# Where the modulation blocks of layer 0 are loaded: two buffers of their own, or these and four of a later stream

## The chip, the cores and the metric

The kernel runs on one core of a Trainium2 chip. The metric is device time in microseconds (us), the median of the runs shown. The engines are TensorE (PE; its weight loads are listed as PEld), VectorE (DVE), ScalarE (ACT), GpSimd (POOL) and SyncE (SP), which here only issues transfers. Each engine, and SP's queue, takes its instructions strictly in the order in which the built program has them.

## The reference

It is a four-layer diffusion transformer on 256 tokens and 256 context tokens of width 2048, in float32. Each layer has a modulation of its own:

```python
def ada_modulation(cond, w, b):
    m = jax.nn.silu(cond) @ w + b          # w: 2048 x 6144 per layer
    return jnp.split(m, 3, axis=-1)        # shift, scale, gate
...
h  = rms_norm(x, norm_g[i]) * (1.0 + scale[:, None, :]) + shift[:, None, :]
hc = rms_norm(ctx, norm_g[i]) * (1.0 + scale_c) + shift_c
...
def fourier_mix(h, w_in, w_out):           # layers 0 and 3
    u, z = jnp.split(h @ w_in, 2, axis=-1)
    ...                                    # 2D FFT of u, times silu(z)
    return y @ w_out
x = x + gate[:, None, :] * o
```

Layer 1 is a windowed attention, layer 2 a convolution block. What matters here is layer 0: no product with its `w_in` can start before the shift and scale of the channels that it contracts over are there, and these need 2048 rows of the modulation matrix.

## The kernel before

**Products.** Matrices are multiplied in split float32: a piece of weights (two row blocks of 128, 512 columns, 512 KB) is loaded into one of two `raw` buffers, ACT writes its high part `whi` (L181), DVE the remainder `wlo` (L182), both in two buffers each, and PE does three matmuls (high by high, high by low, low by high: L194 to L196 where the weights stand still, L214 to L216 where the activations do). Results collect in four PSUM banks named `accz` or `accu`.

**Layer 0, first half (L674 to L728).** The product for z is made in nine steps over the contraction: steps 0 and 1 take one block of 128 channels, steps 2 to 8 two (`steps`, L606). Within a step a loop over four column groups (`cg`) loads one piece, multiplies it into the four banks `accz`, and DVE adds each bank to a sum `y` in SBUF (L726); the next group's matmuls may write a bank only after that. In the last step ACT puts silu on `y` (L728). Then come the 32 pieces of the product for u (`accu`), which starts in the order of its row blocks.

**Layer 0's modulation blocks.** While step j runs, the shift and scale of the channels of step j + 1 are made (`ada_tiles`, L221): in each column group one quarter q of the 2048 rows, 512 rows by 512 columns, 1 MB, is loaded by two transfers (L231) and multiplied by the conditioning vectors (L235, four matmuls on four column strips of the array). After the fourth quarter the sums are turned into columns (L241, L243, L246, L249) and the activations `hh`, `hl` of step j + 1 are built (L448 to L450). The quarters go through two buffers of 1 MB (tile `aw` of the pool `aw0`), which are given back after the last step; step 0 alone puts its second half elsewhere (below).

**The later modulation rows.** All other shifts, scales and gates are made by two streams (`Stream`, L318) from row blocks of 128 rows by 2048 columns, each loaded as two tiles of 512 KB (L331) into four buffers (tile `aw` of the pool `wp`, `AWB` = 4). Stream `ada_v` works on DVE: it multiplies a tile by one number per row and adds it to a running sum `adacc` (L284; the first row block is L282). Stream `ada_a` works on PE (L271). The text of the program starts both in step 8: twelve row blocks (24 tiles) of `ada_v` after the first column group (L721), eight row blocks of `ada_a` in its four groups (L723), and then a part of a row block per piece of the product for u (`pump0`, L731).

**What sets the order.** The program is written as one sequence. A scheduler gives each engine its own order from it; it moves an instruction forward when its inputs and its buffer are free early enough by its own estimate. Buffers of one tile name are handed out in turn in the order of the text. So the 24 tiles of `ada_v`, written in step 8, stand in the queues from step 0 on in the kernel before, since their four buffers have no other user after step 0.

Of the kernel before, what the change touches and what calls it, by code (L numbers as in the profile page):

```python
# [11 lines left out]
F32 = mybir.dt.float32  # L12
# [7 lines left out]
P = 128  # L20
D = 2048
# [39 lines left out]
AWB = 4  # L61
# [7 lines left out]
def dit_kernel(ctx: ExitStack, tc: tile.TileContext, x, c, ctxt, c_ctx, norm_g, ada_w, ada_b,  # L69
               four_w_in, four_w_out, attn_w_in, attn_sink, attn_w_out, conv_w_in, conv_dw_w,  # L70
               conv_dw_b, conv_ln_g, conv_ln_b, conv_w_out, final_g, dft, rope, maskc, out):
    nc = tc.nc
    mm = nc.tensor.matmul
# [3 lines left out]
    wp = ctx.enter_context(tc.tile_pool(name="wp", bufs=1))  # L77
# [11 lines left out]
    def nm(s):  # L89
        uid[0] += 1  # L90
        return f"{s}_{uid[0]}"

    def tmp(shape=(P, 512), dt=F32):
        return wp.tile(list(shape), dt, tag="tmp", bufs=TB, name=nm("tmp"))
# [126 lines left out]
    def ada_tiles(k, n, j, pl, pa):  # L221

        w = 2 * P * n
        for q in range(4):
            if j == 0 and q > 1:
                aw = wp.tile([P, D // 2], F32, tag="aw", bufs=AWB, name=nm("aw"))[:].rearrange("p (k c) -> p k c", k=4)
            else:
                aw = pl.tile([P, 4, 512], F32, tag="aw", bufs=2, name=nm("aw"))
            for i in range(2):
                c0 = (1 - i) * D + P * k  # L230
                nc.sync.dma_start(aw[:, :, i * P * n:(i + 1) * P * n],  # L231
                                  ada_w[0, q * 512:(q + 1) * 512, c0:c0 + P * n].rearrange("(k p) c -> p k c", p=P))
            for g in range(4):
                cs = csil[:, 4 * q + g, :] if q else csil0[:, g, :]
                mm(pa[32 * g:32 * g + cs.shape[-1], :w], cs, aw[:, g, :w],  # L235
                   start=q == 0, stop=q == 3, skip_group_check=True)
            if q < 3:
                yield
        with tc.high_priority(offset=FH if j < FJ else 0):
            a = tmp()  # L240
            nc.scalar.copy(a[:, :w], pa[:, :w])  # L241
            for i in range(2 * n):
                mm(pa[:, 2 * i:2 * i + 2], a[:, i * P:(i + 1) * P], sel[:], start=True, stop=True)  # L243
            for i, c0 in enumerate((16 + k, k)):
                dst = modc[0][:, c0:c0 + n, :]
                nc.vector.tensor_add(dst, pa[:, 2 * n * i:2 * n * (i + 1)].rearrange("p (k o) -> p k o", o=2),  # L246
                                     adabT[:, c0:c0 + n].unsqueeze(2).to_broadcast([P, n, 2]))
                if i == 0:
                    nc.vector.scalar_tensor_tensor(dst, dst, 1.0, ngT[:, k:k + n].unsqueeze(2).to_broadcast([P, n, 2]),  # L249
                                                   op0=ALU.add, op1=ALU.mult)  # L250
        yield
# [356 lines left out]
    def ada_start(j):  # L608
        return ada_tiles(*steps[j], j, aw0, psa_box[0].tile([P, 512], F32, tag="ada", name=nm("pa")))
# [72 lines left out]
    for o in range(2):  # L682
        if o:
            rs[1] = to_channels(1, 512)
        cs = slice(256 * o, 256 * o + 256)
# [105 lines left out]
    for cg in range(4):  # L791
# [9 lines left out]
        if cg == 3:  # L801
            sqrt_table(st.ss[:, 0:1])
            tail = {kt: piece(kt) for kt in range(KT - 4, KT, 2)}
            for o in range(2):
                cs = slice(256 * o, 256 * o + 256)
# [530 lines left out]
```

## Time and profile before

| what | value |
|---|---|
| median of 3 runs | 1928.31 us (1928.18 to 1931.59) |
| the profiled execution, its time | 1930.65 us |
| its span in the trace | 1928.5 us |
| mean granted TensorE clock | 0.986 |
| DVE busy, of the span | 1441.8 us (75%) |
| ACT busy | 892.7 us (46%) |
| POOL busy | 228.0 us (12%) |
| moved by DMA | 433.63 MB, 225 GB/s on average |

The times in the rows count from the start of the span. 2.15 us of the profiled execution's time lie outside of its span. Step 2 of the first half starts at about 71 us, step 8 at about 243 us, the product for u at about 276 us.

A line of the timeline gives start, length, engine, source line, operation, tiles and count, and in square brackets the idle time ahead of it with what ended it. A line of the windows gives, for a stretch, the busy time of each engine, then the granted clock, the busy share of the 16 DMA engines and GB/s. A line of the waits gives engine and line, what it waited for, the sum in us, how often, and the longest. "SPq" rows are SP's queue; DMA landing times run from issue to the last byte.

### The profile page before, as it was taken

Reading aid. Unit: us, or ns where it says so; the run is one execution under the profiler, and the core shown is the slowest. Engines: PE = TensorE matmul, PEld = TensorE weight load, DVE = VectorE, ACT = ScalarE, POOL = GpSimd, SP = SyncE. Lnnn points to the kernel's source line nnn. Section 1 sums busy time; section 2 is a strip of 40 time slices with the busy share of each in tenths; the row PEclk is TensorE's granted clock in tenths of the full one; section 3 lists DMA queues with packets and bytes.
Section 4 is the critical chain, followed back from the end, with each engine's and each line's share of the span. In section 5 each row is a group of like instructions: output and inputs, shape, how many; then the busy total and the mean of one; then the engine's idle time right before and its main releaser. Section 6 shows DMA issues by size and latency. Waiting matters only on the chain.

```text
span 1928.5 us, 30124 instructions
## 1 busy us (share of the span) xinstructions
PE 1852.9 (96%) x11143; PEld 1506.8 (78%) x11143; DVE 1441.8 (75%) x2719; ACT 892.7 (46%) x1606; POOL 228.0 (12%) x127
## 2 busy tenths in 40 slices
PE   6999999999999999999999999899998998999997
PEld 5566657777766787766689887899998887899886
DVE  4899944566654459977897796588899998897675
ACT  6333342224331236465555445444445656556553
POOL 0000000000000000000000002788880002000000
PEclk9999999999999999999999999999998998999999
DMA  8888878666677745831667695476765795876553
GB/s 257 282 297 301 300 245 271 206 232 207 233 269 265 272 151 161 275 120 55 206 208 251 227 320 197 159 232 212 234 230 175 245 322 169 290 273 176 163 175 131
DMA packets 247236, 433.63 MB, mean 225 GB/s; under 512 B 16214, under 2 KB 135734, under 8 KB 247090
## 3 DMA queue, kind: packets, MB, share of 16 engines
q1 hardware_dynamic: 245664, 430.00, 67.5%
q10 hardware_dynamic: 1426, 1.73, 0.3%
q8 instruction: 87, 1.43, 0.3%
q14 instruction: 59, 0.48, 0.1%
HBM read 429.56 MB, written 2.10 MB: 224 GB/s over the span
## 4 chain that ended last, share of the span: by engine, by line
PE 78%; DVE 9%; DMA 6%; issue 3%; ACT 2%; POOL 0%; SPq 0%; DVEq 0%; ACTq 0%; POOLq 0%
PE acco L1040 8%; PE accz L194 6%; PE accz L195 6%; PE accz L196 6%; DMA aw<-in_ada_w_dram 5%; PE acco L1041 4%; PE accu L214 4%; PE accu L215 4%; PE accu L216 4%; PE pa L271 3%; PE accg L194 3%; PE accg L196 3%; PE accg L195 3%; PE acco L194 3%; DVE wlo L182 3%
## 5 line engine op out<-in xcount | busy, mean ns | idle before, releaser
L181 ACT CAST whi<-raw 128x512 fp32r<-128x512 f32 (+1 forms) x764 | 540.8, 758 | 693.0 <-PE accz L195 133.0
L182 DVE TENSOR_TENSOR wlo<-raw,whi 128x512 fp32r<-128x512 f32 x680 | 492.0, 770 | 202.4 <-ACT whi L181 197.7
L182 POOL TENSOR_TENSOR wlo<-raw,whi 128x1024 fp32r<-128x1024 f32 x84 | 203.8, 2434 | 1371.6 <-ACT whi L181 1370.6
L284 DVE SCALAR_TENSOR_TENSOR adacc<-aw,csil,adacc 128x1024 f32<-128x1024 f32 x188 | 243.9, 1302 | 85.7 <-DMA aw<-in_ada_w_dram 85.2
L1040 PE MATMUL acco<-yh,whi 128*128 128x512 f32 x768 | 270.4, 397 | 0.2 <-DVE xT L1048 0.2
L196 PE MATMUL accz<-hx,wlo 128*128 128x256 f32 x768 | 221.1, 289 | 12.1 <-DVE wlo L182 12.0
L195 PE MATMUL accz<-hx,whi 128*128 128x256 f32 x768 | 220.9, 288 | 3.6 <-DVE hx L450 3.6
L194 PE MATMUL accz<-hx,whi 128*128 128x256 f32 x768 | 220.9, 288 | 1.1 <-ACT hx L449 1.1
L1041 PE MATMUL acco<-yh,wlo 128*128 128x256 f32 x768 | 215.2, 280 | 1.2 <-DVE wlo L182 1.2
L1139 DVE SCALAR_TENSOR_TENSOR pv<-gp,dwT,pv 128x256 f32<-128x256 f32 x480 | 191.1, 482 | 24.8 <-ACT pv L1133 24.4
L1040 PEld LDWEIGHTS acco<-yh,whi 128*128 128x128 f32 x768 | 144.1, 188 | 34.6 <-ACT yh L479 0.8
L196 PEld LDWEIGHTS accz<-hx,wlo 128*128 128x128 f32 x768 | 150.1, 196 | 14.1 <-DVE wlo L182 13.1
L195 PEld LDWEIGHTS accz<-hx,whi 128*128 128x128 f32 x768 | 150.3, 196 | 5.4 <-DVE hx L450 4.2
L194 PEld LDWEIGHTS accz<-hx,whi 128*128 128x128 f32 x768 | 150.3, 196 | 3.0 <-ACT hx L449 1.8
L196 PE MATMUL accg<-hx,wlo 128*128 128x256 f32 x512 | 146.6, 286 | 2.8 <-POOL wlo L182 2.7
L194 PE MATMUL accg<-hx,whi 128*128 128x256 f32 x512 | 147.5, 289 | 1.1 <-ACT hx L449 1.1
L1041 PEld LDWEIGHTS acco<-yh,wlo 128*128 128x128 f32 x768 | 144.8, 189 | 2.2 <-DVE wlo L182 2.1
L195 PE MATMUL accg<-hx,whi 128*128 128x256 f32 x512 | 146.4, 286 | 0.0
L194 PEld LDWEIGHTS accg<-hx,whi 128*128 128x128 f32 x512 | 99.6, 195 | 8.5 <-issue 6.9
L194 PE MATMUL acco<-yh,whi 128*128 128x512 f32 (+1 forms) x272 | 105.0, 387 | 0.0
L196 PEld LDWEIGHTS accg<-hx,wlo 128*128 128x128 f32 x512 | 99.6, 195 | 4.3 <-POOL wlo L182 3.4
L195 PE MATMUL acco<-yl,whi 128*128 128x512 f32 (+1 forms) x272 | 102.8, 378 | 0.0
(261 smaller groups left out, 3579.9 us busy)
## 6 DMA issues: line engine op xcount, KB each, us to landing
aw<-in_ada_w_dram SPq DMA_DIRECT2D x376, 512.0 KB, 5.4
raw<-in_four_w_in_dram SPq DMA_DIRECT2D x126, 512.0 KB, 4.6
raw<-in_attn_w_in_dram SPq DMA_DIRECT2D x72, 512.0 KB, 3.6
raw<-in_conv_w_in_dram SPq DMA_DIRECT2D x128, 256.0 KB, 2.9
raw<-in_four_w_out_dram SPq DMA_DIRECT2D x32, 512.0 KB, 6.7
raw<-in_attn_w_out_dram SPq DMA_DIRECT2D x64, 256.0 KB, 4.3
raw<-in_conv_w_in_dram SPq DMA_DIRECT2D x32, 512.0 KB, 4.4
raw<-in_conv_w_out_dram SPq DMA_DIRECT2D x64, 256.0 KB, 4.6
```

Of the source, the lines that this page charges most:

```text
L181: nc.scalar.copy(hv[:, c], iv[:, c])
L182: eng.tensor_sub(lv[:, c], iv[:, c], hv[:, c].bitcast(F32))
L194: mm(o, a, hh, start=st, stop=False, skip_group_check=True)
L195: mm(o, a, hl, start=False, stop=False, skip_group_check=True)
L196: mm(o, b, hh, start=False, stop=kt + k == span[1] - 1, skip_group_check=True)
L214: mm(acc[:], hh, whi[:, k, :], start=st, stop=False)
L215: mm(acc[:], hh, wlo[:, k, :], start=False, stop=False)
L216: mm(acc[:], hl, whi[:, k, :], start=False, stop=kt + k == KT - 1)
L284: ins = nc.vector.scalar_tensor_tensor(acc[:, cs], aw[i][:], cc, acc[:, cs], op0=ALU.mult, op1=ALU.add)
L1040: mm(o[:], whi[:, k, cs], rhs(kt), start=kt == 0, stop=False, skip_group_check=True)
L1041: mm(o[:, :256], wlo[:, k, cs], rhs(kt)[:, :256], start=False, stop=kt == KT - 1, skip_group_check=True)
L1139: nc.vector.scalar_tensor_tensor(pv[:, :256], gt[:, t:t + 256], dwT[:, kt, t:t + 1], pv[:, :256], op0=ALU.mult, op1=ALU.add)
```

## The change

In `ada_tiles` the second half of every step (quarters 2 and 3) now goes into the four 512 KB buffers of the later rows, as step 0's did already; quarters 0 and 1 keep the two buffers of 1 MB. With two channel blocks a quarter takes two of the 512 KB tiles, each loaded by two transfers of 256 KB, so a quarter is four transfers in place of two; with one channel block it still fits in one tile. The matmuls are as many as before and read the tile that holds their row block. No buffer is added.

```diff
         for q in range(4):
-            if j == 0 and q > 1:
-                aw = wp.tile([P, D // 2], F32, tag="aw", bufs=AWB, name=nm("aw"))[:].rearrange("p (k c) -> p k c", k=4)
+            if q > 1:
+                aws = [wp.tile([P, D // 2], F32, tag="aw", bufs=AWB, name=nm("aw"))[:]
+                       .rearrange("p (k c) -> p k c", k=4 // n) for _ in range(n)]
             else:
-                aw = pl.tile([P, 4, 512], F32, tag="aw", bufs=2, name=nm("aw"))
-            for i in range(2):
-                c0 = (1 - i) * D + P * k
-                nc.sync.dma_start(aw[:, :, i * P * n:(i + 1) * P * n],
-                                  ada_w[0, q * 512:(q + 1) * 512, c0:c0 + P * n].rearrange("(k p) c -> p k c", p=P))
+                aws = [pl.tile([P, 4, 512], F32, tag="aw", bufs=2, name=nm("aw"))[:]]
+            r = 4 // len(aws)
+            for h, aw in enumerate(aws):
+                for i in range(2):
+                    c0 = (1 - i) * D + P * k
+                    r0 = q * 512 + h * r * P
+                    nc.sync.dma_start(aw[:, :, i * P * n:(i + 1) * P * n],
+                                      ada_w[0, r0:r0 + r * P, c0:c0 + P * n].rearrange("(k p) c -> p k c", p=P))
...
-                mm(pa[32 * g:32 * g + cs.shape[-1], :w], cs, aw[:, g, :w],
+                mm(pa[32 * g:32 * g + cs.shape[-1], :w], cs, aws[g // r][:, g % r, :w],
                    start=q == 0, stop=q == 3, skip_group_check=True)
```

The change also moves instructions in the queues, since the four buffers now have a user up to the last modulation block of layer 0. Lines behind the diff carry numbers larger by four: L331 is L335, L284 is L288, L726 is L730. Two places are shown here, as the built programs have them; the number behind a tile's name is its own.

SP's queue before, from the last loads of step 7 on: `raw_2065` is the first piece of step 8, `raw_2199`, `raw_2259` and `raw_2319` its other three, `raw_2393` and `raw_2425` the first two pieces of the product for u; `aw` are tiles of later rows.

```order
L157 DMA raw_2065<-in_four_w_in_dram 128x2x512
L331 DMA aw_2164<-in_ada_w_dram 128x1024
L331 DMA aw_2166<-in_ada_w_dram 128x1024
L331 DMA aw_2170<-in_ada_w_dram 128x1024
L331 DMA aw_2172<-in_ada_w_dram 128x1024
L331 DMA aw_2179<-in_ada_w_dram 128x1024
L331 DMA aw_2181<-in_ada_w_dram 128x1024
L157 DMA raw_2199<-in_four_w_in_dram 128x2x512
L157 DMA raw_2259<-in_four_w_in_dram 128x2x512
L157 DMA raw_2319<-in_four_w_in_dram 128x2x512
```

Behind these stand four `aw`, `raw_2393`, four `aw`, `raw_2425`: never more than six tiles of later rows lie between two pieces, and 22 of `ada_v`'s first 24 are ahead of `raw_2065`.

SP's queue of the changed kernel, at the same place of the program: `raw_2107` and `raw_2241` are the first two pieces of step 8, `raw_2301` and `raw_2361` its last two, `raw_2435` and `raw_2467` the first two of the product for u. Between the last two rows stand 30 more loads of L335, `aw_2170` to `aw_2403`, and nothing else.

```order
L157 DMA raw_2107<-in_four_w_in_dram 128x2x512
L335 DMA aw_2139<-in_ada_w_dram 128x1024
L335 DMA aw_2141<-in_ada_w_dram 128x1024
L157 DMA raw_2241<-in_four_w_in_dram 128x2x512
...
L157 DMA raw_2361<-in_four_w_in_dram 128x2x512
L335 DMA aw_2158<-in_ada_w_dram 128x1024
L335 DMA aw_2160<-in_ada_w_dram 128x1024
L335 DMA aw_2164<-in_ada_w_dram 128x1024
L157 DMA raw_2435<-in_four_w_in_dram 128x2x512
L335 DMA aw_2166<-in_ada_w_dram 128x1024
...
L157 DMA raw_2467<-in_four_w_in_dram 128x2x512
```

So the loads of `ada_v` begin with `aw_2139`, behind the first piece of step 8, and 31 tiles of later rows (15 for DVE, 16 for PE) stand between the first and the second piece of the product for u.

DVE before, in step 8, from the remainder of its second piece to that of its third (`accz_2061` to `accz_2064` are the banks of its first column group):

```order
L182 TENSOR_TENSOR wlo_2202<-raw_2199,whi_2201 128x2x128x2 x2
L450 SCALAR_TENSOR_TENSOR hl_355<-tmp_2017,modc_87,hh_354 128x256
L726 TENSOR_TENSOR y_7_363<-accz_2024,y_7_363 128x512
L480 TENSOR_TENSOR dftl_2382<-tmp_2379,dfth_2381 128x512
L726 TENSOR_TENSOR y_0_356<-accz_2061,y_0_356 128x512
L726 TENSOR_TENSOR y_0_356<-accz_2062,y_0_356 128x512
L726 TENSOR_TENSOR y_1_357<-accz_2063,y_1_357 128x512
L480 TENSOR_TENSOR dftl_2382<-tmp_2380,dfth_2381 128x384
L726 TENSOR_TENSOR y_1_357<-accz_2064,y_1_357 128x512
L182 TENSOR_TENSOR wlo_2262<-raw_2259,whi_2261 128x2x128x2 x2
```

DVE of the changed kernel, from the same remainder on (`accz_2103` to `accz_2105` are the first three of these banks):

```order
L182 TENSOR_TENSOR wlo_2244<-raw_2241,whi_2243 128x2x128x2 x2
L730 TENSOR_TENSOR y_7_363<-accz_2066,y_7_363 128x512
L288 SCALAR_TENSOR_TENSOR adacc_2143<-aw_2146,csil,adacc_2143 128x1024
L288 SCALAR_TENSOR_TENSOR adacc_2143<-aw_2148,csil,adacc_2143 128x1024
L288 SCALAR_TENSOR_TENSOR adacc_2143<-aw_2152,csil,adacc_2143 128x1024
L182 TENSOR_TENSOR wlo_2304<-raw_2301,whi_2303 128x2x128x2 x2
L288 SCALAR_TENSOR_TENSOR adacc_2143<-aw_2154,csil,adacc_2143 128x1024
L288 SCALAR_TENSOR_TENSOR adacc_2143<-aw_2158,csil,adacc_2143 128x1024
L288 SCALAR_TENSOR_TENSOR adacc_2143<-aw_2160,csil,adacc_2143 128x1024
L288 SCALAR_TENSOR_TENSOR adacc_2143<-aw_2164,csil,adacc_2143 128x1024
L730 TENSOR_TENSOR y_0_356<-accz_2103,y_0_356 128x512
L730 TENSOR_TENSOR y_0_356<-accz_2104,y_0_356 128x512
```

The multiply-adds of `ada_v`'s first twelve row blocks, which before stand one by one among the work of all steps from step 0 on, now all stand inside step 8, and the additions of its banks stand behind some of them. Behind the second piece of the product for u, the rows of all engines are the same in both programs but for line and tile numbers, up to the end, apart from the places of a few single rows in its first eight pieces.

## The prediction

> **What bounds the kernel now.** I read the page first, then the windows, and then, in the stretch that the change touches, PE's timeline, the waits, SP's timeline and the single lines. The page says that PE is the engine that is nearly always at work:
>
> ```profile
> span 1928.5 us, 30124 instructions
> PE 1852.9 (96%) x11143; PEld 1506.8 (78%) x11143; DVE 1441.8 (75%) x2719; ACT 892.7 (46%) x1606; POOL 228.0 (12%) x127
> ```
>
> The windows of 20 us (busy time of PE, PEld, DVE, ACT, POOL, then granted clock, DMA share, GB/s) show the steps of layer 0, up to about 243 us, and what follows:
>
> ```profile
> 80.00:100.00 20.00, 19.71 (x96) 14.11 (x95) 16.39 (x28) 7.27 (x10) 0.00 (x0) 1.00 0.97 327
> 160.00:180.00 20.00, 19.69 (x100) 13.28 (x99) 18.36 (x25) 6.76 (x7) 0.00 (x0) 1.00 0.91 316
> 240.00:260.00 20.00, 18.65 (x83) 9.78 (x81) 14.84 (x20) 13.13 (x18) 0.00 (x0) 1.00 0.62 203
> 260.00:280.00 20.00, 20.00 (x93) 10.97 (x90) 7.93 (x12) 6.91 (x12) 0.00 (x0) 1.00 0.76 265
> 280.00:300.00 20.00, 20.00 (x95) 14.63 (x94) 6.33 (x8) 3.42 (x6) 0.00 (x0) 1.00 0.74 257
> ```
>
> In the steps PE is full, DVE and DMA nearly so; behind them DVE has room. Now SP's waits up to 345 us, and PE's and PEld's up to 96 us, then the one idle time of PE in a whole step, and (from the chain that ended last) the same matmuls a step later, 28.06 us on:
>
> ```profile
> SPq L231 <- PE pa L235: 98.0, 29, 6.8
> ...
> PE pa L235 <- DMA aw<-in_ada_w_dram: 2.5, 3, 0.9
> ...
> PEld pa L235 <- DMA aw<-in_ada_w_dram: 2.2, 2, 1.3
> ...
> 150.66 1.05 PE L243 MATMUL pa<-sel,tmp 128*128 128x2 f32 x8 [0.33 <-ACT tmp L241]
> ...
> 178.72 1.05 PE pa L243 x8
> ```
>
> SP waits 98.0 us for the two large buffers. But who loses by it is PE, and PE loses little: at most 2.5 + 2.2 = 4.7 us, all before 96 us. Later, from step to step, its only idle time is 0.33 us, and that is for ACT, not for a load. So four places can win at most 4.7 us here, and nothing in steps 3 to 8.
>
> **The change part by part.** *More transfers.* SP's row for one quarter:
>
> ```profile
> 164.08 0.92 SPq L231 DMA_DIRECT2D aw<-in_ada_w_dram  x2
> ```
>
> In seven steps two quarters take four transfers in place of two: 28 more, at 0.92 / 2 = 0.46 us each 13 us of SP, spread over steps in which it waits 98.0 us. I cost it at nothing; if that cover went, a quarter would be asked for 0.9 us later, and only then could PE wait that long for it. That the halves are smaller loads costs nothing either, for the loads of `ada_v` leave these steps.
>
> *Earlier quarters in the first steps.* The wait of 4.7 us may go, or be replaced by PE's next wait, for the activations. Bounds 0 and -4.7 us; I take -2, since the larger part (2.5) is three separate waits and PE's second pass of step 0, fed by the context, sets the start of step 1 beside them.
>
> *The stream that must wait.* This is the cost. The four buffers are handed out in the order of the text, so `ada_v`'s 24 first tiles come behind layer 0's last block, in step 8. There are three queues to look at: SP, DVE, and PE behind both. SP's rows of before, in the same place:
>
> ```profile
> 222.88 10.50 SPq L331 DMA_DIRECT2D aw<-in_ada_w_dram  x6
> 233.47 10.63 SPq L157 DMA_DIRECT2D raw<-in_four_w_in_dram  x3
> 248.94 2.56 SPq L331 DMA_DIRECT2D aw<-in_ada_w_dram  x4
> 251.60 0.38 SPq L157 DMA_DIRECT2D raw<-in_four_w_in_dram  x1
> 256.49 4.32 SPq L331 DMA_DIRECT2D aw<-in_ada_w_dram  x4
> 260.86 0.43 SPq L157 DMA_DIRECT2D raw<-in_four_w_in_dram  x1
> ```
>
> The row at 251.60 is the first piece of the product for u, the row at 260.86 the second: 9.3 us apart. In the changed order 31 tiles of 524,288 bytes (16.25 MB) stand between them, and only four buffers take them. The second piece cannot be asked for before SP has issued all 31. How fast is a buffer turned around? Its tile must land, be used by DVE (or PE), and the next be issued:
>
> ```profile
> L331 SPq DMA_DIRECT2D aw<-in_ada_w_dram x22: 327/334/1176, 248.9 to 297.8; - x22
> DMA to landing us min/median/max: 4.8/6.1/8.3
> ...
> L284 DVE SCALAR_TENSOR_TENSOR adacc<-aw,csil,adacc x28: 1246/1284/1311, 90.7 to 316.2; 128x1024 f32<-128x1024 f32 x28
> ...
> DMA to landing us min/median/max: 3.7/6.8/7.2
> ```
>
> (The first two lines are L331 from 244 to 300 us, the third the multiply-adds, the last the landing of weight pieces from 95 to 300 us.) Least: 4.8 + 1.28 + 0.33 = 6.41 us per buffer, 1.60 us per tile with four. At the median, with 0.47 us (0.92 / 2) per issue: 6.1 + 1.28 + 0.47 = 7.85 us, 1.96 us per tile. The bandwidth alone gives 524,288 bytes / 327 GB/s = 1.60 us, the same as the least. Between the ends I take the middle, 1.78 us: landing is between its least and its median when four are in flight. PE's use of one of the last 16 tiles, 1.03 us in the row at 259.41 below, is near enough to DVE's 1.28.
>
> Where does the run begin and what waits for its end?
>
> ```profile
> 245.69 1.89 DVE L726 TENSOR_TENSOR y<-accz,y 128x512 f32<-128x512 f32 x3 [0.51 <-PE accz L196]
> 248.93 2.15 DVE L182 TENSOR_TENSOR wlo<-raw,whi 128x512 fp32r<-128x512 f32 x2 [0.26 <-ACT whi L181]
> ...
> 249.72 0.50 PE L194 MATMUL accz<-hh,whi 128*128 128x512 f32 x1
> ...
> 259.41 1.03 PE L271 MATMUL pa<-aw,csil 128*2 128x512 f32 x4 [0.28 <-DMA aw<-in_ada_w_dram]
> ...
> 283.38 0.39 PE L216 MATMUL accu<-whi,hl 128*128 128x512 f32 x1
> 283.61 0.39 PE L214 MATMUL accu<-whi,hh 128*128 128x512 f32 x1
> ...
> 266.04 1.12 ACT L181 CAST whi<-raw 128x512 fp32r<-128x512 f32 x2
> ```
>
> Until step 8 nothing has moved on PE but the -2 us. The first load of the 31 waits for the multiply-add behind the remainder that ends at 248.93 + 2.15 = 251.08 us: it is issued at 251.08 + 1.28 = 252.4 us. The second piece is then issued 31 turns later, lands 6.8 us on, and is cast in 1.1 us: 252.4 + 31 x 1.78 + 6.8 + 1.1 = 315.5 us. Before, PE starts it at 283.61 us. So PE is 31.9 us late there. The least: 252.4 + 31 x 1.60 + 3.7 + 1.1 = 306.8 us, 23.2 us late; the most, with 1.96 and 7.2: 321.5 us, 37.9 us late.
>
> Is DVE's queue a second cost, on top? The additions of step 8's first banks end before at 245.69 + 1.89 = 247.6 us and a fourth one later; now four multiply-adds, 5.1 us, and the remainder at 248.93 stand ahead of them, so they come at about 256 us, and PE's second column group, which may not write the banks sooner, starts there and not at 249.72: 6.5 us late. But PE has only three groups and one piece to do, 283.61 - 249.72 = 33.9 us of work before, until the second piece comes at 315.5. 256 + 33.9 = 290: the delay lies under SP's. It counts only if it slows the turns; that is a rival.
>
> Is the time got back later? From there on the queues are those of before, all shifted; PE is full at 20.00 of 20 us in the rows of 260 and 280 us, so a late PE stays late. Steps 0 to 8 do not shrink for the loads that they lose, since PE does not wait for them.
>
> Sum on the profiled execution (1930.65 us, of it 2.15 outside of the span): +31.9 - 2.0 = +29.9, 1960.6 us. The median lies 2.3 us below that execution, so 1928.3 + 29.9 = 1958.2 us. Ends of the known terms: +23.2 - 4.7 = +18.5 (1946.8) and +37.9 (1966.2).
>
> **The rivals.** *Fast turns.* The loads of later rows can run faster than in the row of 327 GB/s, and PE's clock has been lower after long waits:
>
> ```profile
> 24.00:28.00 4.00, 1.59 (x7) 1.30 (x8) 4.00 (x6) 4.00 (x8) 0.00 (x0) 0.81 1.16 318
> 28.00:32.00 4.00, 4.00 (x28) 4.00 (x28) 0.31 (x1) 2.77 (x8) 0.00 (x0) 0.76 0.58 170
> 280.00:285.00 5.00, 5.00 (x24) 4.10 (x23) 0.49 (x1) 1.14 (x2) 0.00 (x0) 1.00 1.03 405
> ...
> 26.16 0.96 PE L695 MATMUL accz<-hh,whi 128*128 128x256 f32 x4 [2.83 <-ACT hh L449]
> 254.17 0.69 DVE L726 TENSOR_TENSOR y<-accz,y 128x512 f32<-128x512 f32 x1 [0.67 <-PE accz L196]
> ```
>
> At 405 GB/s a tile takes 1.29 us, as long as DVE's multiply-add. If landing shrinks with it, the second piece starts at 252.4 + 31 x 1.29 + 3.7 + 1.1 = 297.2, +13.6 - 2 = +11.6: 1939.9 us. Against it: with four buffers this needs a landing of 4 x 1.29 - 1.28 - 0.33 = 3.55 us, and the least in the row is 4.8. The Trainium skill (DMA: Bandwidth & Descriptors, Anatomy of one DMA) fits a transfer that GpSimd issues as 2.0 us plus its bytes at 436 GB/s; a tile would land in 3.2 us and a turn take 1.20 us per tile, the sum coming to about 1937 us, an estimate from that page. The trace does not agree with that rule for SP's loads here: their least is 4.8 us, their median 6.1.
>
> *Locked turns and a slow clock.* DVE stands in order: an addition in front of a multiply-add waits for PE, PE waits for banks that wait for DVE, and buffers meanwhile stay full. Twelve additions of step 8 stand in the run, each waits 0.67 us for PE when DVE is ahead, as in the row at 254.17: 8 us. Around the 2.83 us that PE idled before 26.16 the granted clock was 0.81 and 0.76; four pieces of 24 matmuls at 0.227 us (283.61 - 283.38), 21.8 us, would take 5 us longer at about 0.8. Together +13 on the middle: +42.9, 1971.2 us. It decides if the first multiply-adds behind 256 us find their tiles landed and DVE waiting for PE. The Trainium skill (TensorE: Matmul & The Clock Gate, What's actually happening) has the clock of an idle PE halved after some 3.4 us; the two rows, means over 4 us, would fit, but no run here shows the gate by itself.
>
> *Faster.* DVE could hide the stream behind step 8 (its 24 multiply-adds are 24 x 1.28 = 30.7 us, and from 240 to 300 us it is idle for 60 - 14.84 - 7.93 - 6.33 = 30.9 us), while the first steps gain the 4.7 us: 1923.6 us. It decides at one point: whether the second piece of the product for u is there by 283.61. For that the 31 loads would have to be issued in 283.61 - 1.1 - 3.7 - 252.4 = 26.4 us, 0.85 us each, 616 GB/s, which no row comes near. Only an order on the chip other than SP's written one would allow it.
>
> *No effect.* That the four buffers are not used as the diff says would leave 1928.3 us; the changed order in SP's queue speaks against it.
>
> **How the numbers follow.** Forecast 0.70, fast turns 0.09, locked turns 0.16, faster 0.03, no effect 0.02. The likeliest gives 1958.2 us. Its own ends are 1946.8 and 1966.2; the upper rival takes the range on to 1971, the lower one, at 1940, and the two small ones stay out with 0.14 of the chance; low end 1946, rounded. A measurement of this kernel can tell 0.2% (3.9 us) from no change: slower by more has the forecast and both turns, 0.95, within it 0.02, faster 0.03.
>
> **What would show it.** In the profile of the changed kernel: SP's row of L335 with some 31 loads and no L157 among them, from about 250 to above 300 us; the next L157 at about 308 us; PE idle in front of `whi` or `accu` around it, ten us and more, and in front of `accz` near 250 us; the rows of steps 3 to 8 28 us apart as before; no L335 before 225 us; DVE in the windows before 240 us less busy by some 4 us per 20. Wrong would be: a second piece before 297 us (the turns), a start of step 3 more than 5 us earlier, or a difference that arises behind 330 us, where I claim that nothing changes.

## The result, and the profile after

The changed kernel takes 1958.82 us (median of 4 runs, 1954.24 to 1964.01), the kernel before, beside it, 1929.25 us (4 runs, 1928.18 to 1931.59): ratio 1.0146, 95% interval [1.0129, 1.0163], or 29.6 us more. The forecast was 1958.2 us. The profiled execution took 1959.32 us, with a mean granted clock of 0.979 (before 0.986). From the medians of the kernel before that stand further down, one run of 2146.72 us at a granted clock of 0.796 is left out. From the page of the changed kernel, the span and the busy times:

```profile
span 1957.4 us, 30202 instructions
PE 1864.3 (95%) x11143; PEld 1511.6 (77%) x11143; DVE 1445.1 (74%) x2719; ACT 894.3 (46%) x1606; POOL 227.9 (12%) x127
```

Nothing was added to the work: the same 11143 matmuls, DVE 3.3 us more. The span is 28.9 us longer. The windows of 20 us say where (PE, PEld, DVE, ACT, POOL, granted clock, DMA share, GB/s):

```profile
160.00:180.00 20.00, 19.64 (x99) 13.22 (x98) 14.81 (x23) 7.85 (x10) 0.00 (x0) 1.00 0.77 239
240.00:260.00 20.00, 10.26 (x34) 7.94 (x33) 19.55 (x20) 7.64 (x10) 0.00 (x0) 0.74 0.83 283
260.00:280.00 20.00, 12.11 (x41) 8.13 (x41) 18.29 (x20) 6.17 (x9) 0.00 (x0) 0.83 0.82 294
300.00:320.00 20.00, 14.56 (x53) 6.07 (x52) 2.59 (x4) 2.28 (x4) 0.00 (x0) 0.83 0.86 301
```

Two things are to be seen. In the row from 160 us, which stands for the steps, PE is as full as before while DVE has 14.81 us where it had 18.36, and DMA 0.77 where it had 0.91: the stream has left the steps. From 240 us DVE is full (19.55 and 18.29 us, before 14.84 and 7.93), PE falls to 34 and 41 matmuls (before 83 and 93), and its clock to 0.74 and 0.83. So PE first waits for DVE; in the row from 300 us it waits for tiles of later rows. SP's timeline has the run as it was foretold, 31 tiles and no L157 among them, and the second piece of the product for u behind it:

```profile
225.10 0.82 SPq L335 DMA_DIRECT2D aw<-in_ada_w_dram  x2
...
248.08 0.38 SPq L157 DMA_DIRECT2D raw<-in_four_w_in_dram  x1
249.19 55.59 SPq L335 DMA_DIRECT2D aw<-in_ada_w_dram  x31
304.83 0.44 SPq L157 DMA_DIRECT2D raw<-in_four_w_in_dram  x1
```

55.59 / 31 = 1.79 us per tile. PE's timeline has the idle times and what ended each:

```profile
233.14 1.05 PE L247 MATMUL pa<-sel,tmp 128*128 128x2 f32 x8 [0.30 <-ACT tmp L245]
254.10 0.76 PE L194 MATMUL accz<-hh,whi 128*128 128x512 f32 x1 [9.74 <-DVE y L730]
269.86 0.79 PE L194 MATMUL accz<-hh,whi 128*128 128x512 f32 x1 [5.96 <-DVE y L730]
312.29 1.87 PE L275 MATMUL pa<-aw,csil 128*2 128x512 f32 x4 [3.13 <-DMA aw<-in_ada_w_dram]
314.34 2.08 PE L214 MATMUL accu<-whi,hh 128*128 128x512 f32 x4 [0.17 <-ACT whi L181]
```

The row at 233.14 stands before at 234.85 (178.72 and two steps of 28.06 us more): in this trace step 8 comes 1.7 us earlier. The last row is the second piece, at 314.34 in place of 283.61 us. The waits of PE from 225 to 345 us, in sum, show where it idled on the way there:

```profile
PE accz L194 <- DVE y L730: 17.5, 4, 9.7
PE pa L275 <- DMA aw<-in_ada_w_dram: 7.0, 5, 3.1
```

In the kernel before, the waits for row tiles come to 0.9 us in the same window, and it has none for additions. For the second piece itself PE idled 0.17 us. The chain that ended last still goes through SP's queue there:

```profile
302.98 1.04 PE pa L275 x8
304.02 0.28 SPq L335
...
304.83 8.74 DMA raw<-in_four_w_in_dram
313.67 0.63 ACT whi L181
314.34 2.08 PE accu L214 x4
```

The chain's first row is PE itself: the last loads of the run waited for a buffer that PE's matmuls on row tiles gave back, and PE came to these late because of the additions. And the row at 312.29 shows that PE's own order would have held the piece as long: matmuls of 16 row tiles stand ahead of it, the last of these tiles came at 312.3 us, and PE was done with them at 314.2. So two paths end within 0.2 us of each other. What takes their place when one is removed was the matter of the experiments.

From there on little is won or lost. The weight loads of line L194 in layer 0's second product (the first and the last execution's start stand behind the comma) are late by 32.5 us at their first and 32.1 us at their last, before and after:

```profile
L194 PEld LDWEIGHTS acco<-yh,whi x272: 186/188/192, 507.3 to 722.2; 128*128 128x128 f32 x136
```

```profile
L194 PEld LDWEIGHTS acco<-yh,whi x272: 186/188/192, 539.8 to 754.3; 128*128 128x128 f32 x136
```

The output product of layer 1 starts at 1117.6 in place of 1087.5 us, 30.1 us late, and the span ends 28.9 us late.

The plainest view is the windows of DVE for the multiply-adds of the stream alone (busy time and count, then clock, DMA share, GB/s), up to 225 us and from there to 280, before:

```profile
0.00:225.00 225.00, 25.68 (x20) 0.99 0.86 287
225.00:280.00 55.00, 2.55 (x2) 1.00 0.74 253
```

and after:

```profile
0.00:225.00 225.00, 0.00 (x0) 0.98 0.76 237
225.00:280.00 55.00, 26.19 (x21) 0.84 0.83 289
```

Twenty multiply-adds that were done beside the steps are now done in one stretch of 55 us, and PE's matmuls on the 16 tiles of `ada_a` follow right behind it, from 280 us on.

### The profile page after: what moved, and what is told of

Its sections match the earlier page's. It is cut to its first block, busy times and chain, and to the rows that moved or that the text cites. A ratio compares the mean times of both kernels' runs of the same rounds, so it can differ in the third digit from the quotient of the medians.

```text
span 1957.4 us, 30202 instructions
## 1 busy us (share of the span) xinstructions
PE 1864.3 (95%) x11143; PEld 1511.6 (77%) x11143; DVE 1445.1 (74%) x2719; ACT 894.3 (46%) x1606; POOL 227.9 (12%) x127
## 4 chain that ended last, share of the span: by engine, by line
PE 81%; DVE 8%; DMA 5%; issue 3%; ACT 2%; POOL 0%; SPq 0%; DVEq 0%; ACTq 0%; POOLq 0%
PE acco L1044 9%; PE accz L194 6%; PE accz L195 6%; PE accz L196 6%; PE acco L1045 4%; PE accu L214 4%; PE accu L216 4%; PE accu L215 4%; PE acco L194 3%; PE pa L275 3%; PE acco L195 3%; PE acco L196 3%; PE accg L194 3%; PE accg L196 3%; PE accg L195 3%
## 5 line engine op out<-in xcount | busy, mean ns | idle before, releaser
L288 DVE SCALAR_TENSOR_TENSOR adacc<-aw,csil,adacc 128x1024 f32<-128x1024 f32 x188 | 243.3, 1305 | 75.5 <-DMA aw<-in_ada_w_dram 75.0
L194 PE MATMUL accz<-hx,whi 128*128 128x256 f32 x768 | 220.5, 288 | 1.1 <-ACT hx L453 1.1
L194 PEld LDWEIGHTS accz<-hx,whi 128*128 128x128 f32 x768 | 149.9, 195 | 3.0 <-ACT hx L453 1.8
L194 PE MATMUL accg<-hx,whi 128*128 128x256 f32 x512 | 147.3, 288 | 1.1 <-ACT hx L453 1.1
L194 PE MATMUL accz<-hh,whi 128*128 128x512 f32 x240 | 99.4, 415 | 17.7 <-DVE y L730 17.5
L730 DVE TENSOR_TENSOR y<-accz,y 128x512 f32<-128x512 f32 x128 | 85.8, 692 | 30.1 <-PE accz L196 30.0
L194 PEld LDWEIGHTS accg<-hx,whi 128*128 128x128 f32 x512 | 99.3, 194 | 8.7 <-issue 6.9
L194 PE MATMUL acco<-yh,whi 128*128 128x512 f32 (+1 forms) x272 | 105.1, 387 | 0.0
```

The costliest lines, as they stand in the source:

```text
L194: mm(o, a, hh, start=st, stop=False, skip_group_check=True)
L288: ins = nc.vector.scalar_tensor_tensor(acc[:, cs], aw[i][:], cc, acc[:, cs], op0=ALU.mult, op1=ALU.add)
L730: nc.vector.tensor_add(y, accs[ci][:], y)
```

## The experiments

The theory was that this stretch costs what its tiles take, 1.78 us each in SP's queue, and that PE waits for the second piece behind them. Rivals were the additions of `y` that stand behind multiply-adds on DVE, the slower clock, and the sharing of the buffers as such. In this table "early" counts the multiply-adds of the stream up to 225 us, "then" those from 225 to 280 us, both from the windows; the last addition of step 8 is from DVE's timeline; the loss is against the median of the kernel before on the same chip (1929.48 us beside the first four, 1931.92 beside the next four, 1929.02 beside the last four).

| kernel | early | then | last addition, us | time, us | loss, us | ratio |
|---|---|---|---|---|---|---|
| before | 20 | 2 | 274.8 | 1929.25 | | |
| changed | 0 | 21 | 291.7 | 1958.82 | 29.6 | 1.0146 [1.0129, 1.0163] |
| e1_last | 0 | 21 | 292.6 | 1963.36 | 33.9 | 1.0168 [1.0146, 1.0190] |
| e2_first | 20 | 2 | 273.1 | 1929.79 | 0.3 | 1.0003 [0.9994, 1.0012] |
| e3_to5 | 13 | 9 | 286.8 | 1942.82 | 13.3 | 1.0065 [1.0044, 1.0086] |
| e4_spread | 0 | 0 | 270.8 | 1935.61 | 6.1 | 1.0037 [1.0021, 1.0052] |
| e5_yfirst | 0 | 16 | 259.7 | 1957.63 | 25.7 | 1.0140 [1.0120, 1.0161] |
| e6_to5_yfirst | 13 | 10 | 268.4 | 1948.37 | 16.5 | 1.0084 [1.0062, 1.0106] |
| e7_poolqueue | 0 | 20 | 303.0 | 1962.54 | 30.6 | 1.0160 [1.0138, 1.0182] |
| e8_three_buffers | 0 | 17 | 290.5 | 1995.30 | 63.4 | 1.0333 [1.0315, 1.0351] |
| e9_late_rows | 2 | 18 | 299.3 | 1961.98 | 33.0 | 1.0172 [1.0157, 1.0187] |
| e10_poolqueue_yfirst | 0 | 15 | 261.2 | 1955.67 | 26.7 | 1.0134 [1.0119, 1.0149] |
| e11_no_pe_rows | 0 | 22 | 287.3 | 1956.20 | 27.2 | 1.0137 [1.0120, 1.0153] |
| e12_no_pe_rows_yfirst | 0 | 15 | 262.7 | 1949.86 | 20.8 | 1.0106 [1.0091, 1.0121] |

**One step's use alone (e1_last).** The changed kernel, with the four buffers used in steps 0 and 8 only:

```diff
-            if q > 1:
+            if q > 1 and j in (0, 8):
```

> Only steps 0 and 8 put their second half into the four buffers; steps 1 to 7 use the two large ones as before. SP's queue then has the same 31 tiles of later rows between the first and second piece of the product for u as the changed kernel. Theory (the stream's loads are held back by the last user of the buffers, and stand in SP's queue between two pieces): the whole loss is there, without the 1.7 us that the first steps gained, about 1960 us (1955 to 1966), ratio 1.015 to 1.018. Rival (each step that uses the buffers costs its part, through more and smaller transfers and buffers that are busy): one step of seven, about 1933 us, ratio about 1.002.

The loss is whole, 33.9 us, and SP's run is the same:

```profile
249.67 55.99 SPq L335 DMA_DIRECT2D aw<-in_ada_w_dram  x31
```

Seven fewer steps of sharing win nothing back. It is the last block in the text that puts the stream behind it.

**Only the first steps (e2_first).**

```diff
-            if q > 1:
+            if q > 1 and j < 2:
```

> Only steps 0 and 1 use the four buffers. The stream's loads start again in step 1, as before the change, and at most six tiles stand between two pieces. Theory: no loss, and the gain of the first steps stays: 1927.5 us (1925 to 1930), ratio 0.998 to 1.000, the fifth matmul group of the columns 1 to 2 us earlier. Rival (there is no gain in the first steps; the 1.7 us in the trace came from the stream's loads being out of the way): 1929 us or more.

No difference can be measured, and the stream stands as before (20 early, 2 then). The rival came out: the matmuls that stand at 233.14 us in the changed kernel's trace stand at 234.64 in this one, 0.2 us ahead of the kernel before, and its time shows no gain. So the 1.7 us are not the first steps' doing. Where they come from stays open: e1_last, which shares nothing in steps 1 to 7, has these matmuls at 233.56, and e9_late_rows below, with the stream late, at 236.89.

**Steps 0 to 5 (e3_to5).**

```diff
-            if q > 1:
+            if q > 1 and j < 6:
```

> Steps 0 to 5 use the four buffers, steps 6 to 8 the large ones; the stream starts in step 5, and the longest run of its tiles between two pieces is 12 (31 in the changed kernel, 4 to 6 before). Theory: a run of 12 takes 12 x 1.79 = 21.5 us, of which the two pieces in the raw buffers and the two that are split hide about 18: 0 to 6 us late, 1928 to 1935 us. Rival (loss in proportion to the run, 12/31 of 30.7 us): about 1939 us.

This missed: 13.3 us are lost, more than the rival's 9 or 10, though the run in SP's queue is short and PE never waits for the piece behind it. SP's timeline, and then PE's:

```profile
251.36 22.64 SPq L335 DMA_DIRECT2D aw<-in_ada_w_dram  x12
```

```profile
255.79 0.80 PE L194 MATMUL accz<-hh,whi 128*128 128x512 f32 x1 [8.62 <-DVE y L730]
```

Nine multiply-adds in place of two stand among the additions, the last addition comes 12.0 us later than before, and that is most of the loss. So the additions behind multiply-adds were no small matter under SP's run: they cost by themselves.

**The stream asked for later (e4_spread).** The changed kernel; step 8 asks for no row block of `ada_v`:

```diff
-TZ = 3
+TZ = 0
```

> All steps use the four buffers, but the text gives the stream on VectorE nothing to do in step 8 (one number, TZ, is 0 in place of 3): its 24 first tiles come with the pieces of the product for u, at most eight in a run. The same bytes are loaded and the same multiply-adds done behind step 8 as in the changed kernel. Theory (the order in SP's queue, not the amount that is put off): most of the loss is gone, 1928 to 1936 us. Rival (12.6 MB and 31 us of VectorE more behind step 8 are what costs): 1950 us or more.

As expected, most of the loss goes. What stays, 6.1 us, arises later: the 24 tiles are now loaded beside the product for u, and from 340 to 640 us PE waits for tiles more than before (0.7 us in sum for PE and 2.1 for PEld there; the rows are e4_spread's):

```profile
PE pa L275 <- DMA aw<-in_ada_w_dram: 4.3, 3, 1.6
...
PEld pa L275 <- DMA aw<-in_ada_w_dram: 8.0, 5, 2.5
```

**The additions first (e5_yfirst).**

```diff
-                nc.vector.tensor_add(y, accs[ci][:], y)
+                with tc.high_priority(offset=400 if j == last else 0):
+                    nc.vector.tensor_add(y, accs[ci][:], y)
```

> The changed kernel, with the additions of the last step's accumulators into y given a higher priority in the scheduler, so that they stand ahead of the multiply-adds of the modulation rows on VectorE. In the program's order four pieces of the u projection now stand ahead of the long run of row tiles in SyncE's queue (35 tiles in place of 31), and TensorE's queue has the matmuls of four pieces ahead of the 20 row tiles' matmuls. Theory (the run in SyncE's queue sets the end): the run starts near 251, takes 35 x 1.79 = 63 us, and the fifth piece lands about 9 us behind it, so TensorE starts the fifth piece near 323, where the kernel before has it near 303: 20 us late, 1949 us (1944 to 1954), although TensorE's waits of 9.7 and 6.0 us for the additions are gone. Rival (the additions behind the multiply-adds are the loss, the run is only what stands beside it): with the additions first, 1929 to 1933.

The loss is 25.7 us, on the theory's side, though above its range: the run begins at 262.8 and not at 251 us. PE waits for no addition any more. It waits for the tiles of its own rows (20.2 us in sum), and then for the fifth piece (SP's timeline, then PE's):

```profile
262.79 55.80 SPq L335 DMA_DIRECT2D aw<-in_ada_w_dram  x35
```

```profile
290.86 4.89 PE L275 MATMUL pa<-aw,csil 128*32 128x512 f32 x16 [11.11 <-DMA aw<-in_ada_w_dram]
...
326.02 0.79 PE L214 MATMUL accu<-whi,hh 128*128 128x512 f32 x1 [4.77 <-ACT whi L181]
```

326.0 less the 303 us of the kernel before is 23 us. The rival falls: with the additions out of the way nearly the same loss stands at the run.

**Steps 0 to 5, the additions first (e6_to5_yfirst).** Both edits, of e3_to5 and e5_yfirst.

> Four buffers in steps 0 to 5 only, as in the earlier experiment that measured 1942.8 us, with the additions into y ahead of the multiply-adds. The longest run of row tiles is 21, and three pieces of u stand ahead of it. Theory (that experiment's 13 us came from the additions standing behind multiply-adds, which kept accumulators from coming free, and from the slower clock after the idle time): the loss goes, 1930 us (1926 to 1935); the run of 21 ends near 251 + 21 x 1.79 = 289 and the fourth piece lands near 298, when the kernel before needs it. Rival (the 13 us came from the run of row tiles and the transfers in it): the run is longer than the 12 it had, so 1943 or more.

Theory and expectation fell: 16.5 us are lost, not nearer to none than the 13.3 of e3_to5 alone; the rival's number, 1943 us or more, came out. The additions end early (268.4 us), but the order now has 21 tiles in a run, from 266.8 us, and PE stands behind them, 6.50 us for a piece and 4.8 us in sum for row tiles (SP's timeline, then PE's):

```profile
266.82 40.61 SPq L335 DMA_DIRECT2D aw<-in_ada_w_dram  x21
```

```profile
316.01 0.79 PE L214 MATMUL accu<-whi,hh 128*128 128x512 f32 x1 [6.50 <-ACT whi L181]
```

So e3_to5's loss was the additions' only as long as these stood in front. With the additions out of the way, it came back at the run in SP's queue.

**The pieces in another queue (e7_poolqueue).** The changed kernel, with the first 8 pieces for u issued by GpSimd:

```diff
-    def w_piece(src, deint=False, lo_eng=None, n=2, prio=SPLIT_PRIO):
+    def w_piece(src, deint=False, lo_eng=None, n=2, prio=SPLIT_PRIO, q=None):
...
-            nc.sync.dma_start(raw[:, 0:n, :], src)
+            (q or nc.sync).dma_start(raw[:, 0:n, :], src)
...
-        gemm_N(accs, lambda kt: w_piece(w_rows(wi, kt, cg * 512)), lhs0, range(0, KT, 2), pump0 if cg < 3 else pump3)
+        gemm_N(accs, lambda kt: w_piece(w_rows(wi, kt, cg * 512), q=nc.gpsimd if cg == 0 else None), lhs0, range(0, KT, 2), pump0 if cg < 3 else pump3)
```

> The changed kernel, with the loads of the first 8 pieces of the u projection issued from GpSimd's queue in place of SyncE's, so that no piece stands behind the run of row tiles. The 16 row tiles that TensorE multiplies (the last of them landed at 312.3 in the changed kernel) still stand in TensorE's own queue, now spread among the first two and a bit pieces of u. Theory (the run of row tiles sets the end by whichever queue carries it: SyncE's for the pieces, TensorE's own for the tiles): TensorE goes on past the last of the 16 near 313, with 51 matmuls of u done, where the kernel before was at 292: 21 us late, 1950 us (1945 to 1956). Rival 1 (only the pieces' place in SyncE's queue matters): the second piece is there in time, what stays is the additions behind the multiply-adds, 1941 us (1936 to 1944). Rival 2 (the transfers themselves are too slow for the DMA engines in that stretch): 1957 or more.

No piece stands behind the run, and nothing is won: 30.6 us, above the theory's 21 and far from the 12 of the rival that only SP's queue matters. Rival 2's number came out, but not its reason, for the DMA share is 0.81 to 0.86 in the windows from 240 to 280 us, as in the changed kernel. SP begins the run 6 us earlier, and DVE has five multiply-adds in place of four between the remainder and the first addition, the fifth of which waits 3.54 us for its tile. PE now waits 25.9 us in sum for additions, where it waited 17.5 (SP's timeline, then DVE's and PE's):

```profile
243.13 101.78 SPq L335 DMA_DIRECT2D aw<-in_ada_w_dram  x48
```

```profile
256.10 1.28 DVE L288 SCALAR_TENSOR_TENSOR adacc<-aw,csil,adacc 128x1024 f32<-128x1024 f32 x1 [3.54 <-DMA aw<-in_ada_w_dram]
...
258.13 0.77 PE L194 MATMUL accz<-hh,whi 128*128 128x512 f32 x1 [14.41 <-DVE y L730]
```

**Three buffers (e8_three_buffers).** `AWB = 3` in the changed kernel.

> The changed kernel with three buffers for the row tiles in place of four, in the whole program, to learn what paces a run of row tiles. Theory (a tile waits for its buffer, so the turn is landing plus use over the number of buffers): 4 x 1.79 = 7.2 us round for a buffer, so 7.2 / 3 = 2.4 us a tile in the longest run (22 tiles). Rival (the DMA engines' rate paces it, 512 KB in 1.79 us): about 1.8 us a tile, since with fewer transfers under way each lands sooner. The total time isn't what is asked, since every later stage has three buffers too and the order around the run changes; 1960 to 2000 us by the theory, 1945 to 1960 by the rival.

SP's timeline, and the landing time of the 22 tiles in that run:

```profile
286.84 46.84 SPq L335 DMA_DIRECT2D aw<-in_ada_w_dram  x22
```

```profile
DMA to landing us min/median/max: 4.0/4.6/6.0
```

46.84 / 22 = 2.13 us per tile, between the two numbers. The landing's median is 4.6 us, as in the run of the changed kernel (249 to 305 us: 3.6/4.6/6.4), so fewer tiles under way did not land sooner, which speaks against the rival that the rate of the DMA engines paces the run. A buffer's round is 3 x 2.13 = 6.4 us against 4 x 1.79 = 7.2: with four, a landed tile waits 0.8 us longer for its user. The number of buffers paces it, by less than in proportion. The two runs do not stand at the same place (286 and 249 us), so this is a comparison of unlike stretches and not a proof.

**The old places, but the stream late (e9_late_rows).** The kernel before, with its two large buffers; the first multiply-add stands behind step 7:

```diff
-                nc.vector.tensor_add(y, accs[ci][:], y)
+                ya = nc.vector.tensor_add(y, accs[ci][:], y)
+                if j == JZ - 1 and cg == 3 and ci == 3:
+                    ada_v.behind = ya
```

> The kernel before, with its two large buffers for the steps' own rows left as they are, and one dependency more: the first multiply-add of a row tile stands behind the last addition into y of step 7. So the row tiles that the kernel before loads one by one beside steps 3 to 8 (22 of its 39 up to 280) come only where the changed kernel has them, and 30 of them stand in a row in SyncE's queue ahead of the second piece of u. Theory (the loss is that those early tiles are gone and the same number has to be got through in one go at 1.79 us each): 250 + 30 x 1.79 = 304, the second piece lands near 313, 30 us late, 1958 us (1952 to 1964). Rival (sharing the four buffers between the steps and the stream is what costs): the steps share nothing here, 1929 to 1935.

This settles the cause. No more buffers are shared with the steps than before, and the loss is there, 33.0 us, with the same run in SP's timeline and the same wait of PE for additions; the second piece starts at 317.84 us, again after almost no wait of its own (0.58 us):

```profile
253.63 56.19 SPq L331 DMA_DIRECT2D aw<-in_ada_w_dram  x30
```

```profile
PE accz L194 <- DVE y L726: 13.4, 3, 6.7
```

**Both queues cleared (e10_poolqueue_yfirst).** The edits of e5_yfirst and e7_poolqueue together.

> The changed kernel with both edits at once: the first 8 pieces of u loaded from GpSimd's queue, and the additions into y ahead of the multiply-adds. Neither a piece nor an accumulator waits for the run of row tiles any more (50 tiles in SyncE's queue now); what is left is TensorE's own order, which has the matmuls of 14 row tiles among pieces 6 to 8 of u and of 12 more behind them. Theory (the run of tiles, at 1.6 to 1.8 us each, holds whichever queue carries it): tile 50 lands between 335 and 345, where TensorE in the kernel before has done 8 pieces near 325: 10 to 20 us late, 1945 us (1939 to 1952). Rival 1 (the pieces behind the run in SyncE's queue were the loss): 1929 to 1934. Rival 2 (nothing but the number of tiles asked for in that stretch counts): 1957, as the two edits gave one by one (1957.6 and 1962.5).

26.7 us: above the theory's range, near rival 2. The additions end at 261.2 us, and up to 300 us PE has 127 matmuls of u done, more than the 86 of the kernel before. Then it comes to its own row tiles, which stand in its order between the pieces, and the run goes on to 356 us; the ninth piece, again in SP's queue, comes behind it:

```profile
360.21 3.00 PE L275 MATMUL pa<-aw,csil 128*2 128x512 f32 x8 [3.21 <-DMA aw<-in_ada_w_dram]
363.51 1.20 PE L214 MATMUL accu<-whi,hh 128*128 128x512 f32 x4 [0.29 <-ACT whi L181]
```

PE waits 10.4 us in sum for the tiles up to 375 us; where the rest of the loss arises was not followed.

**No rows for PE in step 8 (e11_no_pe_rows).** `A0Z = 0` in the changed kernel.

> The changed kernel with A0Z at 0 in place of 2: the last step asks for none of the rows that TensorE multiplies (16 tiles), the rows for VectorE stay as they are. The longest run in SyncE's queue is 15 tiles. Theory: the run ends near 250 + 15 x 1.79 = 277 and the second piece is there near 287, 3 us behind the kernel before; what stays is the additions behind the multiply-adds, which cost 13 us where the run was 12 tiles: 1942 us (1936 to 1947). Rival (only the run in SyncE's queue matters): 1929 to 1934. Rival (the number of tiles doesn't matter, the four buffers do): 1957.

27.2 us, 14 us over the expectation. The last addition comes 12.5 us later than before, much as expected. The expectation took e3_to5's 13 us for the additions, but PE idled 8.6 us for them there and 17.4 here. And it went by the start of the second piece, which leaves out the matmuls of the rows that were put off: PE is the bound, and owes them later. The windows from 225 to 360 us for those rows' matmuls alone (L271 before), then for `accu` alone, before:

```profile
225.00:360.00 135.00, 20.48 (x124) 1.00 0.73 248
225.00:360.00 135.00, 68.47 (x288) 1.00 0.73 248
```

and in e11_no_pe_rows (L275, `accu`):

```profile
225.00:360.00 135.00, 10.63 (x64) 0.91 0.76 258
225.00:360.00 135.00, 58.55 (x240) 0.91 0.76 258
```

48 matmuls of u (68.47 less 58.55, 9.9 us) and 60 of the rows (20.48 less 10.63, 9.9 us) are missing, together 19.8 us, and 31 of the transform that follows (tiles `pb` and `pm`), 4.3 us in the same windows. PE's waits in e11_no_pe_rows from 225 to 345 us have the additions as in the changed kernel (17.5 us there):

```profile
PE accz L194 <- DVE y L730: 17.4, 4, 10.1
```

So DVE's order, with a run of only 15 tiles in SP's queue and 5.2 us of waiting for tiles, loses nearly as much as the changed kernel.

**The same, the additions first (e12_no_pe_rows_yfirst).**

> The same with the additions into y ahead of the multiply-adds; the longest run is 21 tiles, ahead of the fifth piece of u, and it starts near 263, as in the other kernel with the additions first. Theory (the tiles asked for in one go cost what they take beyond the work of TensorE that stands ahead of them): the run ends at 263 + 21 x 1.6 to 1.9 = 297 to 303, the fifth piece lands 9 us behind it, at 306 to 312, and TensorE, with 10 tiles' matmuls (10 us) less behind it than the kernel before, comes to it at 295 to 303: 5 to 15 us late, of which the matmuls not yet done are owed later: 1940 us (1933 to 1947). Rival (the additions behind the multiply-adds are all that is left once the 16 tiles are gone): 1929 to 1932.

20.8 us, 3 above the range. PE waits 11.03 and 5.51 us for tiles, and up to 360 us it has done 260 matmuls of u where the kernel before has done 288:

```profile
293.40 4.83 PE L275 MATMUL pa<-aw,csil 128*32 128x512 f32 x16 [11.03 <-DMA aw<-in_ada_w_dram]
```

**What follows.** The loss goes with the tiles that the last step gets through in one go, not with a queue. Only kernels that keep the tiles early (e2_first) or ask for them later (e4_spread) are near the time of before; the one that makes them late without any sharing (e9_late_rows) loses all. Each edit of order cleared the wait it was aimed at, and left 16 to 31 us at the next one: the additions on DVE, the tiles in PE's order, the pieces in SP's queue. No version beats the kernel before.

## Why the prediction was right

- **More transfers.** Costed at nothing. PE's idle time in the step is 0.30 us, as before (0.33). Right.
- **The first steps, -2 us.** The trace has 1.7 us at step 8; e2_first, with this part alone, gains nothing that can be measured. The term was nearer to its end at zero.
- **The turn, 1.78 us per tile.** Measured 1.79, but in part by luck. The landing was shorter than assumed (median 4.6 us, where the working lay between 4.8 and 6.1), and a landed tile waited about a microsecond for its user, which the working had at nothing: 4 x 1.79 = 7.2 us, less 4.6, 1.28 for the use and 0.33 for the issue, leaves 1.0. The two errors cancel. (0.92 / 2 is 0.46 and not 0.47 us, which changes nothing.) The ends, 1.60 and 1.96, were nearly those of some other runs: 55.80 / 35 = 1.59 us in e5_yfirst, 40.61 / 21 = 1.93 in e6_to5_yfirst; above them are e7_poolqueue, 101.78 / 48 = 2.12, and e10_poolqueue_yfirst, 111.56 us for 50 tiles or 2.23.
- **The second piece at 315.5 us,** or 313.5 with the 2 us of the first steps. It started at 314.34: the run began at 249.19 and not at 252.4 us, and the landing of that piece took 8.74 us in place of 6.8.
- **The delay by DVE's order, 6.5 us, "lies under SP's".** This is the step that was wrong. PE idled 9.74 us there, then 5.96 more, 17.5 us in sum, and ran slower behind both; the last addition came 16.9 us late. The prediction had PE through with its own work at 290 us, and idle from there to 315.5. It was through at 314.2, for besides those waits it waited 7.0 us for row tiles, and its order has 64 matmuls of row tiles ahead of the second piece, where the 33.9 us taken from the kernel before hold 48. So the delay filled the whole time that SP's run was to cost. Nearly all of the idle time stands at the additions and the row tiles, and that the sum still fits is in part luck, since two paths end together.
- **SP's queue as the place of the loss.** The run and its length came as foretold, but the sign that went with it, PE idle ten us and more in front of `whi` or `accu`, did not: 0.17 us. Where the additions are put first, PE does wait for a piece, 4.77 us in e5_yfirst and 6.50 in e6_to5_yfirst. e7_poolqueue took the pieces out of that queue and won nothing; e11_no_pe_rows, in which the run is 15 tiles, still loses 27.2 us. The two costs do not stand one under the other as 32 and 6.5; they come from the same tiles, and with either eased nearly the whole loss stays (25.7 us in e5_yfirst, 27.2 in e11_no_pe_rows). That the tiles come late, said in the prediction at *The stream that must wait*, is what e9_late_rows confirms.
- **Locked turns and a slow clock.** The clock did fall, to 0.74 and 0.83, behind the waits for additions; how much of the loss is the clock's, no run separates. The turns did not lock: 1.79 us.
- **Fast turns, faster.** Neither was seen, though the reason given against fast turns was weak: loads did land in less than the 4.8 us that was taken for the least (3.6 us). No run of tiles went below 1.56 us each (32.77 us for the 21 of e12_no_pe_rows_yfirst).
- **Nothing is recovered.** Right within some 4 us: 30.7 us late at the second piece, 32.5 at the start of layer 0's second product, 30.1 at layer 1's output product, 28.9 at the end.

## What to carry to other kernels

A buffer that looks idle beside a stage may be the one that lets a later stream run ahead, hidden under that stage; before it is lent out, count how much of the stream's work, on every engine, loses its cover, and where it will be done in place. When a bunch of work stands in the way of a full engine, reordering one queue only moves the wait to the next one; what helps is fewer items in the bunch, earlier or later. And work that the bounding engine merely puts off is not saved: count what it still owes at the point at which two traces are compared.

## What the runs showed of the hardware

After the 9.74 us in which PE idled, its matmuls were spaced 0.43 us in place of 0.23 for 5.7 us, from PE's timeline of the changed kernel (two of the thirteen slow ones, and the first of the fast):

```profile
254.67 0.63 PE L195 MATMUL accz<-hl,whi 128*128 128x512 f32 x1
255.09 0.63 PE L196 MATMUL accz<-hh,wlo 128*128 128x512 f32 x1
...
260.10 0.40 PE L196 MATMUL accz<-hh,wlo 128*128 128x512 f32 x1
260.33 0.39 PE L194 MATMUL accz<-hh,whi 128*128 128x512 f32 x1
```

That is 13 x 0.2 = 2.6 us on top of an idle time of 9.74. The windows of PE around them (busy time, granted clock, DMA share, GB/s) show the granted clock at half for 10 us:

```profile
244.20:249.50 5.30, 0.17 (x1) 1.00 0.87 278
249.70:259.70 10.00, 5.59 (x13) 0.50 0.98 356
259.90:266.50 6.60, 4.01 (x18) 1.00 0.80 301
```

The Trainium skill (TensorE: Matmul & The Clock Gate, What's actually happening) has an idle PE at half its clock until one activity window of some 3.4 us, which runs on by itself, has been busy. The trace agrees: the clock fell some 5 us after PE had stopped and came back 5.7 us after it had started again, each time between one such window and two.

A tile of 512 KB landed in a median of 4.6 us with three and with four tiles under way, and of 5.2 us in the run of e5_yfirst, the fastest but one. By these figures the pace of a run goes with the buffers and with how soon a tile's user comes to it, more than with how soon it lands.
